# A hybrid decoder block on one core: half of the last weight units get two of their four block sums from an adding DMA

## The chip, the core and the metric

One Trainium2 chip, one core of it. The metric is the device time of the kernel in microseconds (us), median of three runs; one further execution is profiled, and its trace is what is read here. The engines are named as in the profile: PE is TensorE (PEld its weight loads), DVE is VectorE, ACT is ScalarE, POOL is GpSimd, SP is SyncE. A "q" behind a name (SPq, POOLq) is that engine's sequencer, which here issues DMAs.

## The reference, cut to what matters

The block has two token mixers side by side and a convolutional feed-forward part. The change touches the feed-forward part alone:

```python
h = _rmsnorm(x, norm2_g[l])                          # (512, 2048)
up = jnp.einsum('bsd,df->bsf', h, ffn_w_up[l])       # (512, 12288)
up = _causal_dwconv(up, ffn_conv_w[l], ffn_conv_b[l])
gate, val = jnp.split(up, 2, axis=-1)
x = x + jnp.einsum('bsf,fd->bsd', jax.nn.gelu(gate) * val, ffn_w_down[l])
return _rmsnorm(x, final_g)
```

Everything is float32; SEQ is 512, D_MODEL 2048, D_FF 6144.

## The kernel before, in words

**Products in seven.** Each feed-forward matrix product is cut into blocks of 512 x 512 x 256 that are multiplied by a Strassen-Winograd scheme: of each operand's four quarters, sums are formed, and seven block products take the place of eight. `SLOTS` says which of the seven slots of either operand meet in a product, `ORDER` in which order. Each product is itself split in high and low parts (`split`: ACT writes the rounded high part `h`, DVE the rest `l`), and three matmuls (high-high, high-low, low-high) stand for one. So a unit costs 7 products x 2 halves x 3 = 42 matmuls of 128x256.

**Units.** A unit is one 256 x 512 piece of the weights. There are 192 of the up product (24 blocks of 8) and 88 of the down product, 280 in all (`units`; `n_up` is 192). The down product runs over three chunks of the contraction (`CHUNKS`: 8, 8 and 6 units for each of four column blocks); the rest (`TAIL`) is done plainly at the end. Before a chunk its 8, 8 or 6 activation pieces have to be prepared like weights: they were written to DRAM (`ad`, line 819, on POOL's queue) by the up stage and are loaded back. These `Acts` entries are put into the stream among the weights of the 13 units around the start of a chunk (`after`, `spread`).

**The stream.** All entries go through three steps, in one order written out by `prepare`:

- `load` (lines 581 and 604): SP issues the DMA of four quarters (512 KB) into places 4 to 7 of a tile `q` of eight places. `q` has three buffers, so the load of entry k waits until the pair step of entry k-3 has read its buffer.
- `sums` (585 to 587 for weights, 610 to 612 for activations): DVE forms the four sums, one instruction for places 2 and 3 (128x512), one each for places 1 and 0 (128x256).
- `pair` (115 and 116): ACT copies the seven places to `h`, DVE subtracts to get `l`. The tiles `wh` and `wl` have three buffers too, so this waits until PE is done with the unit three before.

Within `prepare`, at entry n, come the load of entry n+2, the sums of n+1 and the pair of n. PE's products of unit u are written out after the pairs of the two units behind it are, so DVE can be some two units ahead.

**Between them**, on DVE: the up blocks combine their seven products (`combine`, lines 769 to 777) and run the convolution (`rest`, 814 to 817); the down blocks add the products to a tile `xs` of the residual, three additions at the end of a block (864, 867, 869) and eight more (871 to 878), two behind each of the next four units (`later`, `lazy`). POOL's queue loads `xs` from DRAM (855) at the second unit of a block and stores it (891) behind the eighth addition. POOL does little else in this stage.

Of the kernel before, what the change touches and what calls it, by code (L numbers as in the profile page):

```python
# [12 lines left out]
ALU = mybir.AluOpType  # L13

P = 128
# [52 lines left out]
def hybrid_block(ctx: ExitStack, tc: tile.TileContext, x, xT, w_in, w_out, w_up, w_dn, w_dl, wab, wsT, vec, bs, vgb, fg, out):  # L68
    nc = tc.nc
# [91 lines left out]
    def project(w, block, act, channel_major, between=None, with_row=None):  # L161

        ps = [bank() for _ in range(4)]

        def load(kc):
            return wchunk(w[block, kc], with_row and (lambda kk: with_row(kc * 4 + kk)))

        ahead = load(0)
        for kc in range(4):
            parts = ahead  # L170
            for i, wt in enumerate(parts):
                for kk in range(2):
                    k = kc * 4 + i * 2 + kk
                    for j in range(4):
                        if channel_major:
                            a, b = sl(wt, slice(None), kk, slice(j * P, (j + 1) * P)), act[k]
                        else:
                            a, b = cols(act[k], j), sl(wt, slice(None), kk, slice(None))
                        mm3(ps[j], a, b, k == 0, k == KT - 1)
            if kc < 3:  # L180
                ahead = load(kc + 1)
            if between is not None:
                between(kc)
        return ps
# [26 lines left out]
    def rms_rstd(dst, sums, width, n):  # L211

        m = sums.shape[-1]
        v = mx.tile([P, n], F32, name="rms_v", tag="rms_v", bufs=2)
        if m > 1:
            nc.vector.tensor_reduce(v, sums, mybir.AxisListType.X, ALU.add)
            sums = v
        else:
            sums = sums[:, :, 0]
        nc.vector.tensor_scalar(v, sums, 1.0 / width, RMS_EPS, ALU.mult, ALU.add)  # L220
        rsqrt(dst, v)
# [348 lines left out]
    def slots(name, n=8):  # L570
        return wq.tile([P, n, 256], F32, name=name, tag=name)

    class Weights:


        def __init__(self, src):
            self.src = src

        def load(self):
            self.q = slots("q")  # L580
            nc.sync.dma_start(self.q[:, 4:8], self.src)

        def sums(self):
            q = self.q
            nc.vector.tensor_tensor(q[:, 2:4], q[:, 5:7], q[:, 7:8].broadcast_to([P, 2, 256]), ALU.add)  # L585
            nc.vector.tensor_tensor(q[:, 1], q[:, 2], q[:, 6], ALU.add)  # L586
            nc.vector.tensor_tensor(q[:, 0], q[:, 1], q[:, 4], ALU.add)  # L587

# [50 lines left out]
    stream = []  # L639
# [18 lines left out]
    n_up = starts[0]  # L658
# [41 lines left out]
    last_w = [Plain([w_dl[d].rearrange("p (a b) -> p a b", a=8)], half_tiles(i)) for i, d in enumerate(DORD)]  # L700
    for u, (src, _) in enumerate(units):
        place[u] = len(stream)
        stream.append(Weights(src))
        for a in after.get(u, ()):
            if a.fill is not None:
                a_place[a.m] = len(stream)
            stream.append(a)
        if u == len(units) - 5:
            stream.append(last_a)
        if u == len(units) - 2:  # L710
            stream.append(last_w[0])
# [195 lines left out]
    for st in range(NS):  # L907
# [22 lines left out]
        v, y, u, r = (const.tile([P, 1], F32, name=f"r3{c}", tag=f"r3{c}", bufs=2) for c in "vyur")  # L930
# [73 lines left out]
```

## Time and profile before

| what | value |
|---|---|
| median of 3 runs | 2142.49 us (2139.59 to 2144.26) |
| profiled execution | 2140.87 us, of which 2139.2 us are the span of the trace |
| busy: PE, DVE, ACT, POOL | 2065.3, 1806.6, 905.5, 59.6 us |
| mean granted TensorE clock | 0.982 |
| loads of weight units | 280 of 512 KB on SP's queue |
| mean DMA rate | 129 GB/s |

The span is the time from the first to the last instruction. Busy times are sums over instructions of one engine; matmuls overlap in the trace, so a busy PE need not be at its full rate, and counts of matmuls in a stretch are the better measure. The up product runs from about 630 to 1595 us, the down product from there to about 2085 us.

### The profile page before, as it was taken

The numbers are of one execution on the slowest core, as the hardware profiler recorded it, in microseconds if no ns is written. First come the engines' busy times: TensorE is split into PE (matmuls) and PEld (weight loads), VectorE is DVE, ScalarE is ACT, GpSimd is POOL, SyncE is SP. The second block draws the span as 40 slices with busy tenths as digits, with TensorE's granted clock in tenths as the row PEclk, the third lists the DMA queues.
The fourth block names the chain that finished last, engine by engine and source line by source line (L and its number), as shares of the span: only waits on it lengthen the run. The fifth ranks groups of instructions, "written<-read, shape, count | busy, mean of one in ns | idle before, by whom it ended". The sixth has DMA issues, their size and how long they took to land.

```text
span 2139.2 us, 34631 instructions
## 1 busy us (share of the span) xinstructions
PE 2065.3 (97%) x14552; PEld 1944.5 (91%) x14552; DVE 1806.6 (84%) x2341; ACT 905.5 (42%) x891; POOL 59.6 (3%) x118
## 2 busy tenths in 40 slices
PE   9999999999789999999999999999988998999998
PEld 7888888888679999999999999999978997998996
DVE  7588972744369999999999999999999999989986
ACT  5445322413244444444444444444444344444443
POOL 0000000100000000000000000000000000000001
PEclk9999999999889999999999999999989999999999
DMA  6222322533013333333333333333335454544563
GB/s 233 87 93 85 112 88 96 172 134 138 40 50 119 116 114 121 117 118 119 119 119 119 119 119 119 119 117 121 119 119 174 149 172 166 179 148 166 197 214 121
DMA packets 68605, 275.14 MB, mean 129 GB/s; under 512 B 8160, under 2 KB 8800, under 8 KB 58720
## 3 DMA queue, kind: packets, MB, share of 16 engines
q1 hardware_dynamic: 57888, 224.01, 32.4%
q0 software_dynamic: 9984, 48.24, 6.1%
q8 instruction: 114, 1.87, 0.4%
q10 hardware_dynamic: 576, 0.66, 0.1%
q14 instruction: 43, 0.35, 0.0%
HBM read 241.43 MB, written 31.46 MB: 128 GB/s over the span
## 4 chain that ended last, share of the span: by engine, by line
PE 47%; issue 39%; DVE 10%; DMA 2%; ACT 1%; POOL 1%; SPq 0%; POOLq 0%; DVEq 0%; ACTq 0%
PE qs L753 18%; PE ps L153 8%; PE ps L151 8%; PE ps L152 8%; DVE wl L116 3%; DVE al L116 2%; POOL ad L819 1%; PE tr L673 1%; DVE q L585 1%; DMA q<-w_dn 1%; PE qs L152 1%; PE qs L153 1%; PE qs L151 1%; DVE q L610 1%; DMA q<-ad 1%
## 5 line engine op out<-in xcount | busy, mean ns | idle before, releaser
L753 PE MATMUL qs<-ah,wh 128*128 128x256 f32 x2688 | 765.1, 285 | 4.9 <-ACT ah L115 2.4
L753 PE MATMUL qs<-ah,wl 128*128 128x256 f32 x2688 | 764.1, 284 | 5.7 <-DVE wl L116 5.7
L753 PE MATMUL qs<-al,wh 128*128 128x256 f32 x2688 | 764.1, 284 | 1.5 <-DVE al L116 1.5
L115 ACT CAST wh<-q 128x1792 fp32r<-128x1792 f32 (+1 forms) x282 | 476.8, 1691 | 669.5 <-PE qs L753 437.4
L116 DVE TENSOR_TENSOR wl<-q,wh 128x1792 fp32r<-128x1792 f32 (+1 forms) x282 | 567.7, 2013 | 24.9 <-ACT wh L115 24.8
L753 PEld LDWEIGHTS qs<-ah,wl 128*128 128x128 f32 x2688 | 519.5, 193 | 6.1 <-DVE wl L116 6.1
L753 PEld LDWEIGHTS qs<-ah,wh 128*128 128x128 f32 x2688 | 519.6, 193 | 5.8 <-ACT ah L115 2.6
L753 PEld LDWEIGHTS qs<-al,wh 128*128 128x128 f32 x2688 | 519.6, 193 | 1.8 <-DVE al L116 1.8
L753 PE MATMUL qs<-wl,ah 128*128 128x256 f32 x1232 | 355.1, 288 | 16.4 <-DVE wl L116 16.4
L753 PE MATMUL qs<-wh,ah 128*128 128x256 f32 x1232 | 354.3, 288 | 9.6 <-ACT cc L863 4.1
L753 PE MATMUL qs<-wh,al 128*128 128x256 f32 x1232 | 353.8, 287 | 4.8 <-DVE al L116 4.8
L753 PEld LDWEIGHTS qs<-wl,ah 128*128 128x128 f32 x1232 | 241.5, 196 | 18.8 <-DVE wl L116 18.7
L753 PEld LDWEIGHTS qs<-wh,ah 128*128 128x128 f32 x1232 | 241.8, 196 | 11.2 <-ACT cc L863 4.5
L753 PEld LDWEIGHTS qs<-wh,al 128*128 128x128 f32 x1232 | 241.6, 196 | 5.2 <-DVE al L116 5.2
L116 DVE TENSOR_TENSOR wl<-wraw,wh 128x1024 fp32r<-128x1024 f32 (+2 forms) x105 | 118.1, 1126 | 147.6 <-ACT wh L115 147.3
L115 ACT CAST wh<-wraw 128x1024 fp32r<-128x1024 f32 (+2 forms) x105 | 102.2, 974 | 275.6 <-PE ps L152 145.3
L585 DVE TENSOR_TENSOR q<-q 128x512 f32<-128x512 f32 x280 | 191.9, 685 | 15.5 <-DMA q<-w_dn 9.2
L151 PE MATMUL ps<-xgh,wh 128*128 128x512 f32 x384 | 152.4, 397 | 1.7 <-ACT wh L115 1.7
L152 PE MATMUL ps<-xgl,wh 128*128 128x512 f32 x384 | 152.1, 397 | 0.0
L153 PE MATMUL ps<-xgh,wl 128*128 128x512 f32 x384 | 150.5, 397 | 0.0
L586 DVE TENSOR_TENSOR q<-q 128x256 f32<-128x256 f32 x280 | 119.0, 425 | 9.7
L587 DVE TENSOR_TENSOR q<-q 128x256 f32<-128x256 f32 x280 | 119.0, 425 | 9.6
(241 smaller groups left out, 2303.9 us busy)
## 6 DMA issues: line engine op xcount, KB each, us to landing
q<-w_up SPq DMA_DIRECT2D x192, 512.0 KB, 3.5
q<-w_dn SPq DMA_DIRECT2D x88, 512.0 KB, 3.5
wraw<-w_in SPq DMA_DIRECT2D x28, 1024.0 KB, 4.9
wraw<-w_out SPq DMA_DIRECT2D x16, 1024.0 KB, 4.9
ad<-gate POOLq DMA_DIRECT2D x48, 256.0 KB, 2.3
q<-ad SPq DMA_DIRECT2D x24, 512.0 KB, 3.2
xs<-x2d POOLq DMA_DIRECT2D x12, 1024.0 KB, 5.7
x2d<-xs POOLq DMA_DIRECT2D x10, 1024.0 KB, 4.7
```

What stands on the lines that cost most here:

```text
L115: nc.scalar.copy(h, src)
L116: nc.vector.tensor_tensor(l, src, h.bitcast(F32), ALU.subtract)
L151: nc.tensor.matmul(ps, lhsT=ah, rhs=bh, start=start, stop=False)
L152: nc.tensor.matmul(ps, lhsT=ah, rhs=bl, start=False, stop=False)
L153: nc.tensor.matmul(ps, lhsT=al, rhs=bh, start=False, stop=stop)
L585: nc.vector.tensor_tensor(q[:, 2:4], q[:, 5:7], q[:, 7:8].broadcast_to([P, 2, 256]), ALU.add)
L586: nc.vector.tensor_tensor(q[:, 1], q[:, 2], q[:, 6], ALU.add)
L587: nc.vector.tensor_tensor(q[:, 0], q[:, 1], q[:, 4], ALU.add)
L610: nc.vector.tensor_tensor(q[:, 2:4], q[:, 7:8].broadcast_to([P, 2, 256]), q[:, 5:7], ALU.subtract)
L673: nc.tensor.matmul(ps[:, st * P:(st + 1) * P], lhsT=x2[k // 4][:, st, (k % 4) * P:(k % 4 + 1) * P], rhs=diag[st], start=True, stop=True)
L753: nc.tensor.matmul(q[p][:, t], lhsT=x_, rhs=y_, start=first and t == 0 and n == 0, stop=last and t == 1 and n == 2, skip_group_check=True)
L819: nc.gpsimd.dma_start(ad[2 * g + n][:, at:at + 2], gate.rearrange("p (a b) -> p a b", a=2))
```

## The change

The weights lie in DRAM in another layout: not four quarters for each row of a unit (4 KB), but seven places (7 KB), in which three quarters stand twice. An ordinary unit loads four of them, in the same order as before, into the same places (a row of 4 KB out of 7 KB). From unit 184 on (the last up block and the whole down product), every odd unit is loaded otherwise: SP brings five places (rows of 5 KB, 640 KB) into places 2 to 6; then a second DMA, on POOL's queue, adds two more places (rows of 2 KB, 256 KB) onto places 2 and 3 in SBUF. This forms the two sums that the first DVE instruction formed, and that instruction (line 585 before) is left out for these units. The other two sums stay on DVE. There are 48 such units: 4 of the up product and 44 of the down product.

```diff
-        def __init__(self, src):
-            self.src = src
+        def __init__(self, src, adds):
+            self.src, self.adds = src, adds
 
         def load(self):
-            self.q = slots("q")
-            nc.sync.dma_start(self.q[:, 4:8], self.src)
+            self.q = q = slots("q")
+            if self.adds:
+
+                nc.sync.dma_start(q[:, 2:7], self.src[:, 0:5])
+                nc.gpsimd.dma_start(q[:, 2:4], self.src[:, 5:7], accum_op=ALU.add)
+            else:
+                nc.sync.dma_start(q[:, 4:8], self.src[:, 2:6])
 
         def sums(self):
             q = self.q
-            nc.vector.tensor_tensor(q[:, 2:4], q[:, 5:7], q[:, 7:8].broadcast_to([P, 2, 256]), ALU.add)
+            if not self.adds:
+                nc.vector.tensor_tensor(q[:, 2:4], q[:, 5:7], q[:, 7:8].broadcast_to([P, 2, 256]), ALU.add)
             nc.vector.tensor_tensor(q[:, 1], q[:, 2], q[:, 6], ALU.add)
             nc.vector.tensor_tensor(q[:, 0], q[:, 1], q[:, 4], ALU.add)
...
-        stream.append(Weights(src))
+        stream.append(Weights(src, u >= n_up - 8 and u % 2 == 1))
...
-        return c(np.stack([b[:, :, :, 0, 1], b[:, :, :, 0, 0], b[:, :, :, 1, 1], b[:, :, :, 1, 0]], axis=3))
+        return c(np.stack([b[:, :, :, n, k] for n, k in ((0, 0), (1, 1), (0, 1), (0, 0), (1, 1), (1, 0), (1, 0))], axis=3))
```

The adding DMA writes what the first DMA has to have written, so POOL's sequencer waits for the landing of the first before it issues the second; the sums on DVE wait for both.

## The prediction

> **What bounds the kernel.** First the page: busy shares, then the slices.
>
> ```profile
> PE 2065.3 (97%) x14552; PEld 1944.5 (91%) x14552; DVE 1806.6 (84%) x2341; ACT 905.5 (42%) x891; POOL 59.6 (3%) x118
> PE   9999999999789999999999999999988998999998
> DVE  7588972744369999999999999999999999989986
> ```
>
> PE is the engine of this kernel, but from slice 12 on VectorE is nearly as full, and PE dips where the down product begins. Next the windows, in stretches whose second column is PE's busy time with the count of matmuls, the fourth VectorE's. The first row is the undisturbed up stage.
>
> ```profile
> 1100.00:1150.00 50.00, 50.00 (x419) 50.00 (x419) 48.47 (x64) 21.92 (x17) 2.16 (x4) 1.00 0.37 117
> 1550.00:1662.00 112.00, 94.73 (x711) 92.68 (x711) 104.49 (x129) 51.67 (x41) 3.23 (x6) 0.91 0.42 141
> 1662.00:1735.00 73.00, 73.00 (x611) 73.00 (x610) 66.72 (x86) 30.14 (x24) 2.13 (x4) 1.00 0.51 174
> 1735.00:1836.00 101.00, 89.03 (x701) 87.16 (x700) 95.07 (x117) 44.44 (x32) 2.13 (x4) 0.97 0.50 165
> 1930.00:2004.00 74.00, 65.99 (x517) 64.93 (x516) 70.52 (x90) 32.67 (x25) 2.13 (x4) 0.95 0.55 185
> ```
>
> 419 matmuls in 50 us are 8.38 a us, so a unit of 42 takes PE 5.0 us. By that rate 1550 to 1662 should hold 939 matmuls and holds 711 (27 us lost), 1735 to 1836 holds 701 of 846 (17 us), 1930 to 2004 holds 517 of 620 (12 us). These three stretches are where activations are prepared among the weights. They are the only places of the stage where VectorE's work can be worth anything, 56 us together; in between (third row) PE is at full rate. That VectorE holds PE there, and is hardly ever held itself, is in the waits (engine, line, releaser: total us, times, longest), the first two for the whole run, then one in the first stretch and one in the second.
>
> ```profile
> PE qs L753 <- DVE wl L116: 22.2, 13, 4.5
> DVE q L585 <- DMA q<-w_up: 5.5, 5, 2.3
> DVE q L585 <- DMA q<-w_dn: 1.8, 1, 1.8
> DVE q L585 <- DMA q<-w_dn: 1.8, 1, 1.8
> ```
>
> The waits of 2.3, 1.8 and 1.8 us stand before units that the change touches (191, 203, 233).
>
> **What is removed.** 48 times the instruction of line 585.
>
> ```profile
> L585 DVE TENSOR_TENSOR q<-q 128x512 f32<-128x512 f32 x280 | 191.9, 685 | 15.5 <-DMA q<-w_dn 9.2
> ```
>
> It lasts 0.685 us, and the next instruction starts 0.72 us after it (below, 1629.15 to 1629.87). 22 of the 48 lie in the stretches (units 189 to 205, 221 to 233, 253 to 263): 22 x 0.72 = 15.8 us. The other 26 lie where PE sets the pace and give nothing by themselves.
>
> **What is added on the path.** The question is when the sums of a changed unit can start. Two rounds of the stream, in the timeline (start, duration; the SPq row is the load):
>
> ```profile
> 1627.22 2.02 DVE L116 TENSOR_TENSOR wl<-q,wh 128x1792 fp32r<-128x1792 f32 x1
> 1629.15 0.68 DVE L585 TENSOR_TENSOR q<-q 128x512 f32<-128x512 f32 x1
> 1629.26 0.33 SPq L581 DMA_DIRECT2D q<-w_dn  x1
> 1629.87 0.42 DVE L586 TENSOR_TENSOR q<-q 128x256 f32<-128x256 f32 x1
> 1630.67 2.02 DVE L116 TENSOR_TENSOR al<-q,ah 128x1792 fp32r<-128x1792 f32 x1
> 1632.73 0.69 DVE L585 TENSOR_TENSOR q<-q 128x512 f32<-128x512 f32 x1
> ...
> 1796.42 0.33 SPq L581 DMA_DIRECT2D q<-w_dn  x1
> 1797.03 0.69 DVE L874 TENSOR_TENSOR xs<-xs,cc 128x512 f32<-128x512 f32 x1
> 1799.16 2.02 DVE L116 TENSOR_TENSOR wl<-q,wh 128x1792 fp32r<-128x1792 f32 x1
> 1801.09 0.68 DVE L585 TENSOR_TENSOR q<-q 128x512 f32<-128x512 f32 x1
> ```
>
> A load is issued the moment a subtract has freed its buffer (1627.22 + 2.02 = 1629.24), and VectorE comes to that unit's own sums one set of sums and one subtract later: 3.5 us after the issue for unit 199, 4.7 us for unit 229, which has two steps of a down block's end (one is shown) in between. Call this time S; it is all the time that the transfers have. By S the 22 units, their own DMA waits taken off, fall into: 3 of about 3.5 (191, 199, 233); 9 of about 4.67 (193, 221, 223, 229, 231, 253 to 257, 261); 6 of 5.1 to 5.6, mean 5.33 (197, 201, 225, 227, and the first and last shown here); 3 of about 5.95 (203, 205, 263, shown); one of 8.1 (195).
>
> ```profile
> 1556.15 0.33 SPq L581 DMA_DIRECT2D q<-w_up  x1
> 1561.26 0.69 DVE L585 TENSOR_TENSOR q<-q 128x512 f32<-128x512 f32 x1
> ...
> 1961.37 0.33 SPq L581 DMA_DIRECT2D q<-w_dn  x1
> 1966.51 0.69 DVE L585 TENSOR_TENSOR q<-q 128x512 f32<-128x512 f32 x1
> ...
> 1982.98 0.33 SPq L581 DMA_DIRECT2D q<-w_dn  x1
> 1988.98 0.68 DVE L585 TENSOR_TENSOR q<-q 128x512 f32<-128x512 f32 x1
> ```
>
> Against S stands R, the time from the first issue to the landing of the adding transfer. The DMA issues (size, median us from issue to landing):
>
> ```profile
> q<-w_dn SPq DMA_DIRECT2D x88, 512.0 KB, 3.5
> q<-w_dl SPq DMA_DIRECT2D x4, 1024.0 KB, 4.8
> ad<-gate POOLq DMA_DIRECT2D x48, 256.0 KB, 2.3
> graw<-wab POOLq DMA_DIRECT2D x8, 128.0 KB, 2.4
> xs<-x2d POOLq DMA_DIRECT2D x12, 1024.0 KB, 5.7
> ```
>
> The first load grows from 512 to 640 KB: between 3.5 and 4.8 a quarter of the way, 3.8 us. POOL then has to see it land and issue; I allow 0.2 us. No adding transfer is in the trace. Its lower end is the 2.3 us of the 256 KB store. The line through POOL's loads of 128 KB (2.4) and 1024 KB (5.7) gives 2.9 us at 256 KB and 3.8 us at 512 KB, if reading the destination counts like another 256 KB. I take 3.0, near the 256 KB load, the row most like it. R is 7.0; its ends are 3.5 + 0.2 + 2.3 = 6.0 and, with a 1 MB transfer beside it (5.7), 9.7.
>
> The page "Collectives: The Full Stack" of the Trainium skill, section "The bandwidth ceiling: the fold count and why AG ≠ RS ≠ AR", says that an add in the DMA is slower by its second source read, not by the arithmetic. With the fit of the Trainium skill's page "DMA: Bandwidth & Descriptors", section "Anatomy of one DMA — SWDGE (gpsimd) path", 2.0 us plus bytes at 436 GB/s, that would be an estimate of 3.2 us against 2.6 for a plain copy; R by these is 7.2 or 6.6, and the sum below would be about 35 or 20 us. No run here shows which.
>
> **The sum.** VectorE stands R - S idle before each changed unit and has nothing else to do, since its order is fixed: behind the wait are the subtract of the unit before, then everything else, and PE waits for that subtract. At R = 7.0: 3 x 3.5 + 9 x 2.33 + 6 x 1.67 + 3 x 1.05 = 44.7 us of waits. Off go the 15.8 us of removed work and the 5.9 us of waits that stand there now: +23 us. The same with R = 6.0 gives 23.5 - 21.7 = +2 us, with 8.0 66 - 21.7 = +44.
>
> Then the reserve. Between the stretches VectorE runs ahead of PE, as far as this (a subtract for unit 219 that ends at 1742.04, the unit's first matmul at 1748.12) and waits only for ACT's copy, 10.4 us in all after 1550:
>
> ```profile
> 1740.02 2.02 DVE L116 TENSOR_TENSOR wl<-q,wh 128x1792 fp32r<-128x1792 f32 x1
> 1748.12 0.28 PE L753 MATMUL qs<-wh,ah 128*128 128x256 f32 x1
> DVE wl L116 <- ACT wh L115: 10.4, 11, 3.0
> ```
>
> Waits of changed units there (S 3.4 to 6.9) eat into this 6 us first, then into what the next stretch starts with. By the same sum seven units before the second stretch cost some 5 us net, nine before the third some 7; taking off what VectorE idles there (2 and 5 us of the 10.4) leaves 3 + 2 = 5 us for PE. Near the end unit 279 has S of 3.5: its 3.5 us are partly taken up by later idling, 1.5 us. Total 22.9 + 5 + 1.5 = +29 us.
>
> **Costed at nothing.** Ordinary loads read 4 KB out of 7 KB rows; the cover is that VectorE waits for the 192 loads of `w_up` 5.5 us in all (the row above). If the cover is gone, each costs what it lands past S. POOL's queue: the `xs` load of a block, issued early today, comes to stand behind the adding transfer of the block's fifth or sixth unit. The shortest room is in a block of six (256 to 261), from the load of unit 261 to the first use of `xs`:
>
> ```profile
> 1974.74 0.33 SPq L581 DMA_DIRECT2D q<-w_dn  x1
> 1995.89 0.68 DVE L864 TENSOR_TENSOR xs<-xs,qs 128x512 f32<-128x512 f32 x1
> POOL x2d L891 <- DVE xs L878: 345.2, 10, 49.0
> ```
>
> That is 21 us for 3.8 + 0.2 + 5.7 us, and at most 3.0 more behind the adding transfer itself. The store waits for the eighth addition with adding transfers behind it, but the next of those belongs to a load issued after that addition's unit, so it still waits for its load. So 48 more issues on POOL cost nobody anything; were that room gone, a block's end would wait up to 5.7 us.
>
> **Rivals.** (a) *The chain is in time* (faster). If both transfers take R of 5.0, the waits fall to 3 x 1.5 + 9 x 0.33 = 7.5 us: 14 us gained, 2128. It turns at R = 5.9, where waits equal the 21.7. For it: nothing but that R is not in the trace; against it: even the lower ends sum to 6.0. (b) *No change*: R from 5.7 to 6.1, within 4 us, 2143. For it: the store's 2.3 us. (c) *The adding transfers are starved*: descriptors wait for VectorE. If each waits out one subtract of 2.02 us, R is 9.0, 87.6 - 21.7 = +66, the reserve is gone, some +29: 2237. Against it: POOL's stores land in 2.3 us with VectorE 48 of 50 us busy. The Trainium skill's page "SBUF — State Buffer", section "SBUF: two separate sides", has this as a trap: a VectorE operation in a two-port mode keeps GpSimd from writing descriptors. The instructions here have two sources; the trace so far does not bear it out.
>
> **How the numbers follow.** The forecast, R from 6.1 to 8, has 0.70; (c) and other slow transfers 0.07; (b) 0.11; (a) 0.12. The sum is against the profiled 2140.87 us: 2170; the median of the runs is 1.6 us above it, 2172. 0.2% is 4.3 us, about what runs of this kernel can tell from no change. R = 8 gives +44, +10 of reserve, +2 at the end: 2198, rounded to 2200. The low end leaves out most of (a): 2138.
>
> **What would show it.** Right: 48 POOL issues `q<-w_dn` and `q<-w_up` of 256 KB landing in about 3 us; waits of VectorE for that DMA before the first sum left to a changed unit, some 2 us each, about 45 us in the stretches; fewer matmuls a us there, full rate between. Wrong: those waits short or gone, or VectorE's waits there with PE not later.

## The result, and the profile after

The changed kernel takes 2298.49 us (median; 2291.77 to 2301.28) against 2142.18 us of the kernel before: 1.0729 times, 95% interval 1.0705 to 1.0752. That is 156 us slower, where 30 were forecast and 2200 us was the upper end of the range. The direction was right and the size was not.

The page after, its busy shares and slices:

```profile
PE 2106.9 (92%) x14552; PEld 1977.3 (86%) x14552; DVE 1774.4 (77%) x2293; ACT 902.9 (39%) x891; POOL 101.4 (4%) x166
PE   9999999998799999999999999997788778877878
DVE  7588854553599999999999999997866675666666
```

VectorE has 32 us less to do and is less full than before; from slice 27 on neither engine is full. Something else paces both. The waits (engine, line, releaser: total us, times, longest) name it. Line 592 is the first sum that a changed unit still has:

```profile
DVE q L592 <- DMA q<-w_dn: 203.6, 44, 7.6
DVE q L592 <- DMA q<-w_up: 11.0, 4, 5.8
PE qs L759 <- DVE wl L116: 111.3, 41, 6.2
```

All 48 changed units make VectorE wait, 4.5 us each on average, and PE then waits for VectorE. One round, unit 209, far from any activations (in the timeline; the last row is the unit's first remaining sum):

```profile
1708.72 2.02 DVE L116 TENSOR_TENSOR wl<-q,wh 128x1792 fp32r<-128x1792 f32 x1
1710.77 0.33 SPq L583 DMA_DIRECT2D q<-w_dn  x1
1712.17 2.02 DVE L116 TENSOR_TENSOR wl<-q,wh 128x1792 fp32r<-128x1792 f32 x1
1715.41 0.85 POOL L584 DMA_DIRECT2D q<-w_dn  x1 [11.35 <-DMA q<-w_dn]
1719.97 0.43 DVE L592 TENSOR_TENSOR q<-q 128x256 f32<-128x256 f32 x1 [5.78 <-DMA q<-w_dn]
```

The load goes out as the subtract ends, as foreseen; VectorE is through with its other work at 1714.19; POOL issues the adding transfer 4.64 us after the load was issued, and VectorE starts 4.56 us after that. So the room (the prediction's S: from the issue of the load until VectorE could have begun the sums) was 3.4 us, and the chain (its R: from the same issue until the adding transfer has landed) 9.2. The DMA issues show its parts (size, median us to landing):

```profile
q<-w_dn SPq DMA_DIRECT2D x44, 640.0 KB, 4.0
q<-w_dn POOLq DMA_DIRECT2D x44, 256.0 KB, 4.7
ad<-gate POOLq DMA_DIRECT2D x48, 256.0 KB, 2.3
```

Over all 48 the chain has a median of 9.5 us (8.4 to 12.2). The medians of its parts are 4.0 for the load, 0.6 until POOL issues and 4.7 for the adding transfer; their means, 4.05, 0.64 and 4.99, add up to the mean chain of 9.7. Last the windows, where the second column is PE's busy time with its matmuls. The first row is the up stage; the second lies for the most part between two stretches, where PE ran at 8.38 matmuls a us before; the third is the second stretch:

```profile
1100.00:1150.00 50.00, 50.00 (x419) 50.00 (x419) 48.48 (x64) 21.35 (x17) 2.16 (x4) 1.00 0.36 117
1690.00:1785.00 95.00, 78.06 (x609) 76.23 (x608) 55.47 (x70) 27.39 (x23) 8.70 (x12) 0.96 0.54 158
1785.00:1905.00 120.00, 85.00 (x604) 82.57 (x603) 83.78 (x101) 40.49 (x27) 8.21 (x11) 0.86 0.50 155
```

609 matmuls in 95 us are 6.4 a us: the parts between the stretches, where the change was to cost almost nothing, lose a quarter of their rate.

### The profile page after: what moved, and what is told of

It reads as the page before. It is cut to its first block, busy times and chain, and to the rows that moved or that the text cites. A ratio compares the mean times of both kernels' runs of the same rounds, so it can differ in the third digit from the quotient of the medians.

```text
span 2296.6 us, 34738 instructions
## 1 busy us (share of the span) xinstructions
PE 2106.9 (92%) x14552; PEld 1977.3 (86%) x14552; DVE 1774.4 (77%) x2293; ACT 902.9 (39%) x891; POOL 101.4 (4%) x166
## 5 line engine op out<-in xcount | busy, mean ns | idle before, releaser
L759 PE MATMUL qs<-wl,ah 128*128 128x256 f32 x1232 | 371.9, 302 | 104.3 <-DVE wl L116 104.2
L759 PE MATMUL qs<-wh,ah 128*128 128x256 f32 x1232 | 368.3, 299 | 36.1 <-ACT wh L115 14.1
L759 PE MATMUL qs<-wh,al 128*128 128x256 f32 x1232 | 365.7, 297 | 2.5 <-DVE al L116 2.5
L759 PEld LDWEIGHTS qs<-wl,ah 128*128 128x128 f32 x1232 | 254.9, 207 | 113.1 <-DVE wl L116 112.9
L592 DVE TENSOR_TENSOR q<-q 128x256 f32<-128x256 f32 x280 | 119.0, 425 | 222.6 <-DMA q<-w_dn 203.6
L759 PEld LDWEIGHTS qs<-wh,ah 128*128 128x128 f32 x1232 | 254.1, 206 | 40.3 <-ACT wh L115 15.6
L759 PEld LDWEIGHTS qs<-wh,al 128*128 128x128 f32 x1232 | 255.2, 207 | 2.9 <-DVE al L116 2.9
L591 DVE TENSOR_TENSOR q<-q 128x512 f32<-128x512 f32 x232 | 158.7, 684 | 6.8 <-DMA q<-w_up 4.3
```

The costliest lines, as they stand in the source:

```text
L759: nc.tensor.matmul(q[p][:, t], lhsT=x_, rhs=y_, start=first and t == 0 and n == 0, stop=last and t == 1 and n == 2, skip_group_check=True)
```

## The experiments

**1. The removal without the chain.** The adding transfer is left out.

```diff
                 nc.sync.dma_start(q[:, 2:7], self.src[:, 0:5])
-                nc.gpsimd.dma_start(q[:, 2:4], self.src[:, 5:7], accum_op=ALU.add)
```

> Leaves out the adding transfer: the 48 units load 640 KB, form only the two later sums on VectorE, and places 2 and 3 hold one quarter each instead of a sum. So it has the gain of the change without its chain. Theory (the chain of two transfers is all of the loss, VectorE's work is worth what was reckoned): 15.8 us and a little at the end are gained, 2122 to 2130. Rival (VectorE's 0.7 us are worth nothing, something else paces the stretches): 2138 to 2146. Rival (the 640 KB loads or the 7 KB rows already cost): above 2150.

2135.92 us, ratio 0.9967 (0.9955 to 0.9978): 7.8 us faster, half of what was reckoned, between the ranges of the theory and of the first rival and in neither. So the adding transfer with its wait makes all of the loss, and the removed work is worth less than its time in the stretches. VectorE's waits after 1500 us, in this kernel and then in that of the second experiment, which removes nothing:

```profile
DVE wl L116 <- ACT wh L115: 23.4, 26, 3.0
DVE q L590 <- DMA q<-w_dn: 14.5, 13, 2.2
DVE q L591 <- DMA q<-w_dn: 9.6, 7, 3.0
DVE q L615 <- DMA q<-ad: 3.8, 2, 2.7
...
DVE q L591 <- DMA q<-w_dn: 12.9, 13, 2.4
DVE wl L116 <- ACT wh L115: 9.7, 8, 3.0
DVE q L616 <- DMA q<-ad: 3.0, 2, 1.8
DVE q L591 <- DMA q<-w_up: 1.3, 2, 1.1
```

Of 48 x 0.72 = 34.6 us, 14 went into waiting for ACT's copy (23.4 against 9.7: parts where PE sets the pace) and 11 into waiting for loads (27.9 against 17.2). The second was not foreseen, and in the trace it has two parts. Some 7 us stand before the unchanged even units (14.5 in line 590, against 7.6 for the same units in the other kernel): a load has the room of one set of sums and one subtract, so whoever shortens the sums takes the room from the load of the next entry, which needs its 3.5 us as before. Some 4 us stand before the changed units themselves (10.2 against 6.7), whose 640 KB land in 4.0 us instead of 3.6.

**2. The layout alone.**

```diff
-        stream.append(Weights(src, u >= n_up - 8 and u % 2 == 1))
+        stream.append(Weights(src, False))
```

> Only the new layout: all units load four of seven places (rows of 4 KB out of 7 KB), no unit is changed otherwise. Theory: no cost, 2138 to 2147, loads of 512 KB land in 3.5 us. Rival: rows with gaps cost some tenths of a us a load, which shows in the stretches: 2150 to 2160.

2145.23 us, ratio 1.0010 (1.0001 to 1.0019). Loads of `w_up` keep 3.5 us. The rows with gaps cost 1.5 us in all, nothing to speak of.

**3. Copy in place of add.** The second transfer overwrites instead of adding.

```diff
-                nc.gpsimd.dma_start(q[:, 2:4], self.src[:, 5:7], accum_op=ALU.add)
+                nc.gpsimd.dma_start(q[:, 2:4], self.src[:, 5:7])
```

> The second transfer copies instead of adding (same rows, same queue, same waits; places 2 and 3 hold a quarter instead of a sum). In the changed kernel it takes 4.7 us from issue to landing. Theory (the adding is what makes it long: it reads its destination too): the copy lands in about 2.9 us, the chain falls from 9.5 to 7.7 us, 48 waits shorten by 1.8 us each: 2205 to 2225. Rival (POOL's queue is slow for any transfer into the tile, or starved): it lands in 4.3 us or more and the time is 2280 to 2300.

2245.98 us, ratio 1.0481 (1.0465 to 1.0497), between the ranges of theory and rival. From its DMA issues:

```profile
q<-w_dn POOLq DMA_DIRECT2D x44, 256.0 KB, 3.8
```

The copy lands in 3.8 us, not 2.9 (2.9 is its shortest of 48; the add's shortest is 3.9). So the adding costs 0.9 us at the median, of which 0.3 is POOL's issue (0.85 against 0.54 us), and a plain transfer at this place is as much longer than foreseen. The mean chain is 8.55 against 9.67 us; 52.5 us of time for 1.12 us is 47 us for each us, almost one for one for 48 units.

**4. A shorter first load.** The 640 KB load in two parts, and the adding transfer waits for the 256 KB alone.

```diff
-                nc.sync.dma_start(q[:, 2:7], self.src[:, 0:5])
+                nc.sync.dma_start(q[:, 2:4], self.src[:, 0:2])
+                nc.sync.dma_start(q[:, 4:7], self.src[:, 2:5])
                 nc.gpsimd.dma_start(q[:, 2:4], self.src[:, 5:7], accum_op=ALU.add)
```

> The same sums as the changed kernel, but the 640 KB load is cut in two, places 2 and 3 first (256 KB), then 4 to 6 (384 KB); the adding transfer waits for the first alone. Theory (time goes by the length of the chain, 1 us of it for each of 48 units): the first load lands about 1 us earlier, so the chain is 8.5 us and the time falls by some 45 us: 2245 to 2265. Rival (the chain is not what sets the time, but the adding transfers' traffic or POOL's queue is): 2285 to 2305.

2256.76 us, ratio 1.0529 (1.0510 to 1.0548), as the theory had it.

```profile
q<-w_dn SPq DMA_DIRECT2D x44, 256.0 KB, 2.7
q<-w_dn POOLq DMA_DIRECT2D x44, 256.0 KB, 4.8
```

The mean chain is 8.63 us, and 41.7 us of time for 1.04 us is 40 for each. The sums and the bytes are those of the changed kernel; only the wait is shorter, and SP has one more issue a unit. It is the length of the chain that sets the time.

**5. Half the bytes.** The transfer adds onto place 2 alone.

```diff
-                nc.gpsimd.dma_start(q[:, 2:4], self.src[:, 5:7], accum_op=ALU.add)
+                nc.gpsimd.dma_start(q[:, 2:3], self.src[:, 5:6], accum_op=ALU.add)
```

> The adding transfer has half its bytes: 128 KB in rows of 1 KB onto place 2 alone (place 3 keeps one quarter instead of a sum). In the changed kernel it took 4.7 us at the median and the whole chain 9.5. Theory (a fixed part of some 3.5 us, the rest by bytes): it lands in about 4.1 us, the chain is 8.9, and at the 45 us of time for each us of chain that the copy and the cut load showed the time is 2262 to 2280. Rival (all fixed): 4.7 us and 2290 to 2300. Rival (mostly by bytes): under 3.5 us and under 2250.

2261.88 us, ratio 1.0550 (1.0535 to 1.0566); the transfer lands in 4.0 us at the median.

```profile
q<-w_dn POOLq DMA_DIRECT2D x44, 128.0 KB, 4.0
```

So 128 KB of adding are 0.7 us, and the line through the two sizes leaves a fixed part that is estimated at some 3.3. The mean chain is 8.87 us; 36.6 us of time for 0.80 us is 46 for each.

**6. The sum on GpSimd's arithmetic.** The changed units load as before, and POOL adds.

```diff
+                nc.sync.dma_start(q[:, 4:8], self.src[:, 2:6])
+                nc.gpsimd.tensor_tensor(q[:, 2:4], q[:, 5:7], q[:, 7:8].broadcast_to([P, 2, 256]), ALU.add)
```

> The same sum on GpSimd's arithmetic instead of a transfer: the 48 units load four quarters (512 KB) as before, then POOL forms places 2 and 3 as soon as the load has landed (its instructions of 128x512 took 1.29 us at the end of the kernel). Chain 3.6 + 0.6 + 1.3 = 5.5 us, near the room that most units have. Theory (time goes by the chain's length): 2135 to 2155. Rival (GpSimd and VectorE get in each other's way in the tile memory): POOL's instruction takes 2 us or more, or VectorE's grow, and the time is 2160 or more.

2146.48 us, ratio 1.0013 (1.0003 to 1.0022). From the groups:

```profile
L592 DVE TENSOR_TENSOR q<-q 128x256 f32<-128x256 f32 x280 | 118.9, 425 | 38.8 <-POOL q L584 30.8
L584 POOL TENSOR_TENSOR q<-q 128x512 f32<-128x512 f32 x48 | 83.5, 1739 | 382.9 <-DMA q<-w_dn 306.2 <-DMA q<-w_up 35.8 <-DVE wl L116 19.3
```

POOL's instruction takes 1.74 us on average (1.29 at the quiet end of the kernel before) and follows the landing by 0.2 us, not 0.6; with the load's mean of 3.9 the chain is 5.8 us. VectorE waits 30.8 us for POOL and is spared 34.6. That nothing is gained is due to the rival too. Line 592 keeps its 0.425 us, but 17 other instructions of VectorE that began while POOL's ran took 1.05 to 1.8 us instead of 0.69 or 0.75. One of them, with POOL's, in the timeline:

```profile
1705.07 2.02 DVE L116 TENSOR_TENSOR wl<-q,wh 128x1792 fp32r<-128x1792 f32 x1
1706.24 2.00 POOL L584 TENSOR_TENSOR q<-q 128x512 f32<-128x512 f32 x1 [6.69 <-DMA q<-w_dn]
1707.00 1.78 DVE L879 TENSOR_TENSOR cc<-cc 128x512 f32<-128x512 f32 x1
```

POOL's begins while a subtract runs and takes 2.00 us; VectorE's next begins while POOL's runs, ends 0.5 us after it, and has 1.78 us for 0.68 us of work. In all VectorE is busy 1792.3 us, 18 more than the changed kernel (1774.4) with the same instructions.

**7 and 8. The sums ahead of time.** Adding transfers form the sums in DRAM during the up stage, and the units load them. First the same two sums for the 44 odd units of the down product, then all four for 39 units among the activations, odd and even, whose VectorE sums fall away altogether.

```diff
+    pre = {u: tc.dram_tile([P, 2, 256], F32, name=f"pre{u}") for u in range(n_up, len(units)) if u % 2 == 1}
...
+        jobs.append(lambda u=u: nc.gpsimd.dma_start(pre[u], units[u][0][:, 0:2]))
+        jobs.append(lambda u=u: nc.gpsimd.dma_start(pre[u], units[u][0][:, 5:7], accum_op=ALU.add))
...
-                nc.sync.dma_start(q[:, 2:7], self.src[:, 0:5])
-                nc.gpsimd.dma_start(q[:, 2:4], self.src[:, 5:7], accum_op=ALU.add)
+                nc.sync.dma_start(q[:, 4:7], self.src[:, 2:5])
+                nc.sync.dma_start(q[:, 2:4], pre[self.u])
```

> The same two sums by adding transfers, but formed in DRAM during the up stage, long before they are needed, for the 44 changed units of the down product (a copy and an add of 256 KB each on POOL's queue); the units then load 256 + 384 KB by SP and have no chain. Theory (the chain was all of the loss, and what is left of the gain is what the kernel without the adding transfer showed, some 8 us): 2130 to 2139. Rival (the extra transfers disturb the up stage, whose loads have some 2 us of room): 2146 or more.

2139.45 us, ratio 0.9981 (0.9972 to 0.9991), half a us above the theory's range. Adding transfers of the same size, here into DRAM and far ahead of their use, make no chain and no loss; what is left is half of the small gain of experiment 1.

> All four sums formed ahead in DRAM (a copy and three adding transfers for each of 39 units of the down product, those among the activations); these units load 512 + 384 KB and have no sums on VectorE, so its subtract never waits behind a load. Theory (taking one of the three sums gave little because the next loads' room shrinks with it, 3.5 us of load against 2.7 us of VectorE's work; taking all three removes that wait from VectorE's order): most of the 56 us that PE loses in the three stretches come back, 2090 to 2115. Rival (loads bound the stretches whatever VectorE does): 2130 or more.

2137.37 us, ratio 0.9972 (0.9960 to 0.9984). The time is in the rival's range, but its cause is not the rival's. The windows and one wait say why; the first window is in the up stage (1669 matmuls before), the others are, by the clock, in the second and third stretch (352 and 342 before):

```profile
800.00:1000.00 200.00, 193.10 (x1578) 191.18 (x1577) 183.65 (x232) 85.77 (x70) 38.52 (x53) 0.99 0.69 186
1750.00:1800.00 50.00, 50.00 (x419) 50.00 (x419) 43.72 (x46) 27.50 (x23) 1.06 (x2) 1.00 0.72 256
1950.00:2000.00 50.00, 50.00 (x419) 50.00 (x418) 42.80 (x45) 26.00 (x21) 1.08 (x3) 1.00 0.76 280
DVE q L591 <- DMA q<-w_up: 43.6, 29, 3.5
```

In these windows the stretches are back at full rate, and the up stage lost about as much: 271 matmuls fewer from 700 to 1540 us, which are 32 us. Its loads came late (the last row; 5.5 us before) beside the transfers of 512 KB that POOL, held by nothing, sent down to 0.5 us apart. In experiment 7 POOL sent 256 KB pieces as closely, and the same up window holds 1665 matmuls at nearly the same DMA rate (180 against 186 GB/s); so the size of the pieces may matter more than their closeness.

**9 and 11. Where the loss is made.** Changed are first the 26 units before, between and behind the stretches, then the 22 within.

```diff
-        stream.append(Weights(src, u >= n_up - 8 and u % 2 == 1))
+        stream.append(Weights(src, u % 2 == 1 and (184 <= u < 189 or 206 < u < 220 or 234 < u < 252 or u > 264)))
```

> Changed are only the 26 of the 48 units that lie between and behind the stretches in which activations are prepared (185, 187, 207 to 219, 235 to 251, 265 to 279); the 22 within the stretches are as before. The prediction costed these 26 at some 5 us, in reserve. At the measured chain of 9.6 us and rooms of 3.4 to 8 us each stands some 4 us, less 0.7 for the removed instruction. Theory (the reserve of 6 us is used up by the first two or three units, the rest goes to PE): 45 to 75 us lost, 2188 to 2218. Rival (VectorE has idle time there that takes the waits in, and all of the loss is made within the stretches): 2145 to 2165.

2224.74 us, ratio 1.0382 (1.0366 to 1.0397): 82 us lost, more than either range has. The first part between two stretches (819 matmuls before), and the wait:

```profile
1662.00:1760.00 98.00, 85.51 (x685) 83.89 (x684) 63.50 (x79) 30.77 (x24) 8.19 (x11) 0.98 0.53 152
DVE q L592 <- DMA q<-w_dn: 114.4, 24, 7.5
```

> The counterpart: changed are only the 22 units within the three stretches (189 to 205, 221 to 233, 253 to 263). Theory (each unit costs its own wait wherever it stands, so the two parts add up): the loss of all 48, some 155 us, less the 82 us of the 26 between: 2209 to 2222. The prediction's own sum with a chain of 9.7 us gives 81 us, 2224. Rival (the parts share a reserve, so that each alone costs less than its share): below 2200.

2223.90 us, ratio 1.0374 (1.0357 to 1.0391): 81 us lost, 2 us above the theory's range and what the prediction's own sum gives. The two parts add up to 163 us, near the 156 of all 48; were a reserve shared, the parts would add up to less than the whole, so neither leans on the other's.

**10. Sums ahead, paced.** All four sums for 30 units, in pieces of at most 256 KB, and POOL reads a column of each unit's tile before it sends the next piece.

```diff
             prepare(ready(u0 + m))
+            if u0 >= 8 and ahead_sums:
+                nc.gpsimd.tensor_copy(pace, stream[place[u0 + m]].hl[0][:, 0, 0:1].bitcast(F32))
+                ahead_sums.pop(0)()
```

> All four sums ahead in DRAM again, for 30 units (192 to 199, 220 to 230, 252 to 262), in pieces of at most 256 KB, one piece for each unit of the up stage: POOL reads one column of a unit's tile first, so it cannot run ahead and send them in bursts. Theory (without pacing the stretches gained some 40 us, and the up stage lost 35 because bursts of 512 KB transfers made loads late): the up stage keeps its 419 matmuls in 50 us, the stretches win 25 to 35 us, 2108 to 2122. Rival (any such traffic delays the loads of the up stage): 2130 or more.

2110.29 us, ratio 0.9845 (0.9828 to 0.9861): 33 us faster than the kernel before, faster than any other here, and as the theory had it. One window in the up stage, then the three stretches in the windows of the prediction's first table:

```profile
1000.00:1200.00 200.00, 199.78 (x1665) 199.59 (x1665) 191.34 (x243) 91.12 (x76) 56.32 (x83) 1.00 0.61 161
1550.00:1662.00 112.00, 102.15 (x808) 100.29 (x807) 105.11 (x123) 55.89 (x44) 7.10 (x12) 0.97 0.59 191
1735.00:1836.00 101.00, 97.53 (x796) 96.92 (x795) 91.33 (x101) 48.13 (x35) 2.14 (x4) 0.98 0.64 217
1930.00:2004.00 74.00, 74.00 (x619) 74.00 (x618) 71.12 (x83) 35.58 (x30) 2.14 (x4) 1.00 0.63 214
```

808, 796 and 619 matmuls stand where 711, 701 and 517 stood, and the up stage is as good as whole (1665 of 1669). The windows are by the clock, and by the third the units run some 20 to 30 us earlier than before; the third stretch itself, from 1905 to 1975 us here, holds 586 matmuls in 70 us, the full rate. Pieces, pace and number of units changed together against experiment 8, so which of them saved the up stage is not shown; after experiment 7 the smaller pieces may have been enough.

## Why the prediction was wrong, by its own steps

**What held.** The bound was read rightly: VectorE's fixed order in three stretches, loads issued when a subtract frees a buffer, and the time S until the unit's sums. The formula for the 22 units in the stretches held too: with R at 9.7 us, the mean chain, it gives 103 - 21.7 = 81 us, and experiment 11, with these units alone, lost 81 us. That 9.7 us is also the prediction's upper end for R is luck: that end was added up from a 1 MB transfer, not from an adding one. Luck, too, is experiment 6's coming out unchanged near the turning point of 5.9 us: there VectorE's instructions were 18 us longer, which the prediction's sum does not have. The layout and POOL's longer queue cost nothing, as costed: VectorE waits for no `xs` load after the change, though these now land in 7.7 us instead of 5.7.

**The first step that failed: the size of R.** Taken was 3.8 + 0.2 + 3.0 = 7.0 us, measured are 4.0 + 0.6 + 4.7. The load was nearly right. POOL's 0.2 us were allowed without a row and are 0.6. The adding transfer was put near a plain load by the line through transfers of other sizes; it is 4.7 us at the median, 1.7 more, and 5.0 on average. Experiment 3 parts the median: 0.9 us are the adding, 0.8 a plain transfer at this place. The shortest copy, 2.9 us, is what the line gave. Why the usual copy is longer stays open: the next unit's load runs beside nearly all of them. For the adding transfers the trace has a hint: the 19 beside which a load went out with them or after them took 5.6 us on average, the 28 whose neighbour had gone out earlier 4.6; for the copies there is no such difference (3.9 and 3.9). The prediction had 9.7 us as the end of R and still cut its range at R = 8.

The Trainium skill's page "Collectives: The Full Stack", section "The bandwidth ceiling: the fold count and why AG ≠ RS ≠ AR", puts the cost of an add on its second read. Experiments 3 and 5 neither show nor refute it: beside the issue the adding of 256 KB costs 0.6 us, and 128 KB of adding are 0.7 us against 0.5 on the prediction's line of plain loads, but no run parts the read from the arithmetic. The 3.2 us worked out from the Trainium skill's page "DMA: Bandwidth & Descriptors", section "Anatomy of one DMA — SWDGE (gpsimd) path", were under even the shortest add, 3.9 us.

**The second: the reserve.** The 26 units before, between and behind the stretches were charged 5 us, and 1.5 for unit 279, on the ground that VectorE runs up to 6 us ahead there. Experiment 9 puts them at 82 us, half of all. A unit there has much the same room S as one in the stretches, 3.3 to 7 us but for units 185 and 187 (about 8), because S is counted in VectorE's own work and not in its lead over PE. And the lead is not there when it is needed. Take unit 206, at the start of the first part between two stretches. The first two lines are its subtract and its first matmul in the kernel before; the others, from experiment 9, are VectorE's first wait for a changed unit of that part (207) and PE's wait for unit 206:

```profile
1679.39 2.02 DVE L116 TENSOR_TENSOR wl<-q,wh 128x1792 fp32r<-128x1792 f32 x1
1682.60 0.28 PE L753 MATMUL qs<-wh,ah 128*128 128x256 f32 x1
...
1683.57 0.43 DVE L592 TENSOR_TENSOR q<-q 128x256 f32<-128x256 f32 x1 [4.15 <-DMA q<-w_dn]
1686.45 0.39 PE L759 MATMUL qs<-wl,ah 128*128 128x256 f32 x1 [0.86 <-DVE wl L116]
```

Before, the lead here was 1.2 us, and it took until unit 215 to grow to 6.1. The first wait used it up. It is not regained: by the third row of the prediction's first table (66.72 of 73 us) VectorE has 0.4 us to spare for each unit, 0.9 for a pair, and 0.7 more by the removed work, against waits of 4.5. So the prediction's own sum, without any reserve, holds for these 26 units as well. Over the rooms of the trace before it gives 102.4 - 18.7 = 84 us at 9.7, where experiment 9 lost 82. At R = 7 it would have given 16 us instead of 6.5, a small error; at R = 9 it gives 66, where the prediction's rival (c) had 29.

**The third: the gain.** For the removed work in the stretches 15.8 us were put down. Without the adding transfer, experiment 1 measured 7.8 us for all 48 units, since part of what is spared goes into waits for loads and for ACT. In the changed kernel this step did not fail: VectorE sets the pace throughout, and the accounts close with all 34.6 us of removed work.

VectorE waited 218 us after the change (203.6 + 11.0 + 2.2 and some small ones) and 25 before for loads and ACT (10.4 + 9.2 + 3.2 + 2.5) in the same stage. The difference less 34.6 us of removed work makes 158, and the spans differ by 2296.6 - 2139.2 = 157 us. PE's own busy time rose by 42 us for the same 14552 matmuls (2106.9 against 2065.3), at a mean granted clock of 0.962 against 0.982. This does not come on top: VectorE waits for ACT's copy, and through it for PE, only 1.2 us in this stage.

**The rivals.** (a) and (b) fell with R. (c) came nearest in size, by another cause: descriptors starved by VectorE would not explain unit 209, where VectorE stands idle from 1714.19 on and the transfer issued at 1715.41 still takes 4.56 us. And the adding transfers of units 185, 187 and 195, during which VectorE was busy for 3.1 to 3.5 us, took 4.0 to 4.1 us, among the shortest of all. The trap on the Trainium skill's page "SBUF — State Buffer", section "SBUF: two separate sides", is thus not what made it long; no run here shows it. What experiment 6 shows held up is GpSimd's arithmetic, not its transfers.

## What to carry to other kernels

In an ordered stream with few buffers, a transfer has the time that the consumer's own work takes between two uses of its buffer. A second transfer chained behind the first has to fit in the same time, and here its excess was paid by every unit, also where the consumer seemed to have a lead: ask how large that lead is at the moment of the first wait, and how fast it grows back. Work taken from the consumer shortens that room for the next load, so taking a part of it gained less than its time, and taking the whole step out of the consumer's order gained more. Adding transfers paid here where they ran far ahead of their use, in pieces of at most 256 KB held to the pace of the kernel; whether the size or the pace kept them from delaying the loads beside them was not parted.

## What the runs showed of the hardware that was not expected

- An adding transfer of 256 KB on POOL's queue takes 4.7 us at the median (3.9 at best), one of 128 KB 4.0, a copy of 256 KB 3.8 (2.9 at best); POOL is held 0.85 us by the issue of the adding one, 0.54 by a copy's.
- Between the landing of SP's load and POOL's dependent DMA issue lie 0.6 us at the median (experiments 3 to 5 too); GpSimd's dependent addition in experiment 6 began 0.2 us after the landing.
- GpSimd's 128x512 addition and VectorE's instructions held each other up in experiment 6: GpSimd's took 1.27 to 3.06 us (1.29 at the quiet end of the kernel before), longest where a subtract of 2.02 us was running when it began, and 17 instructions of VectorE that began during one took 1.05 to 1.8 us instead of 0.69 or 0.75.
